# SSD mixer: the normalised residual formed on VectorE instead of GpSimd, and both mask products of the first group in banks of the smaller PSUM pool

## The chip, the core and the metric

The kernel runs on one core of a Trainium2 chip. The core has a matrix engine (TensorE, "PE" in the profile; its weight loads are "PEld"), VectorE ("DVE"), ScalarE ("ACT"), GpSimd ("POOL") and SyncE ("SP"), whose queue issues nearly all DMAs here. Each engine takes its own queue of instructions strictly in the order in which they stand; an instruction that waits holds up everything behind it on that engine. The metric is the device time of one execution in microseconds (us), lower is better.

## What is computed

A trunk of two layers on 512 tokens of width 1024. Each layer is: half a gated feed-forward block, a mixer, a second half block, and a gated embedding. The mixer of layer 0 is a bidirectional SSD (state-space) scan, that of layer 1 is neighbourhood attention. The change lies in the SSD mixer, cut here to what matters:

```python
def ssd_mixer(h, w_in, conv_w, conv_b, dt_bias, a_log, d_skip, norm_g, w_out):   # h = rmsnorm(residual, mix_norm)
    proj = h @ w_in
    z, xbc, dt_raw = jnp.split(proj, [SSD_D_INNER, SSD_D_INNER + SSD_CONV_DIM], axis=-1)
    xbc = jax.nn.silu(centred_depthwise_conv(xbc, conv_w, conv_b))
    xs, b_f, c_f, b_b, c_b = jnp.split(xbc, ...)
    dt = jax.nn.softplus(dt_raw.reshape(bsz, seqlen, 2, SSD_HEADS) + dt_bias)
    y_fwd = ssd_scan(xs, dt[:, :, 0], a[0], grp(b_f), grp(c_f))
    y_bwd = flip(ssd_scan(flip(xs), flip(dt[:, :, 1]), a[1], flip(grp(b_b)), flip(grp(c_b))))
    ...
# in ssd_scan, for each chunk of 128 tokens:
    cb = jnp.einsum('bcqgn,bckgn->bcqkg', cc, bc)                       # the mask products
    scores = cb[..., None] * jnp.exp(jnp.where(lower, seg, -jnp.inf))
```

## The kernel before

Activations stand with features on the partitions: the residual `h` is eight tiles of 128 x 512 (tiles `hs`). An fp32 product is made of three matmuls of rounded parts, high x high (line 278), high x low (281), low x high (282). So every operand is kept as two parts. An activation becomes a pair in a tile `md` by `split()` (lines 301 to 309): a rounded copy on ACT (303, or 306 with a gain) and the remainder on DVE (304, or 307 with a gain). A weight unit of 128 x 1024 is loaded into `wr` by SP, rounded into `wh` by ACT (221), and its remainder goes into `wl` by DVE (223); `wh` and `wl` have three buffers each, and a unit is prepared three products ahead of its use. `gemm()` takes a unit and eight pairs: 24 matmuls of 512 columns into one PSUM bank.

The SSD mixer (`ssd`) first makes the product for dt and the first one of `project(0)` from pairs that carry the gain but not yet the norm's factor, since that factor R (tile `rt`, ACT's copy at line 359) is only known a little later. R is multiplied in afterwards (681 for dt, 748 for the first three products). At the same time the loop at line 685 forms the normalised residual `xn`, which all later projections read: `t` = residual x R on GpSimd (687), then `split()` with the gain (306 on ACT, 307 on DVE), eight times.

`project(gi)` makes eight products for each of eight groups: six go through a convolution (752, four times 756, 759, 760) into `bt`, `ct_` and `xt`, two through a gate (780, 781). `steps()` turns the dt product into step sizes: a transpose on PE (696), a chain of small operations of 256 elements on DVE with two on GpSimd between them (700 to 712), cumulative sums on PE (716, 721), copies on ACT, two more transposes (733), and rows written out to DRAM (`crow`, `vrow`, 738 and 739) that `expo()` reads back (797) for the exponents (800, 803).

`scan(gi)` runs beside the projections of the next group: it transposes tokens (834, copied by ACT at 837), makes the mask products of both directions (845, four matmuls of 128 x 128 each into one bank), multiplies them by the mask on DVE (848), and goes on to the states and the output.

PSUM's eight banks are two pools: `mm` with five and `px` with three. A product waits until the last reader of its bank is done. Before, the mask products took a bank of `mm` for the first direction and one of `px` for the second.

The order of each engine's queue is fixed when the program is built: the framework takes instructions by their place in the code, by dependencies and free buffers and by its own estimates of when things are ready; the code adds a few hints (`issue_after`, `keep_in_program_order`). So an edit in one line can change the order around it on every engine.

Of the kernel before, what the change touches and what calls it, by code (L numbers as in the profile page):

```python
# [11 lines left out]
ALU = mybir.AluOpType  # L12
# [58 lines left out]
def trunk(ctx, tc, A, out):  # L71
    nc = tc.nc
    v, s, g, te, sy = nc.vector, nc.scalar, nc.gpsimd, nc.tensor, nc.sync
# [25 lines left out]
    def md(dt=F32):  # L99
        return bp.tile([P, 2, T], dt, name=nm("md"), tag="md", bufs=24)  # L100
# [7 lines left out]
    def bank(tag, bufs):  # L108
        return ps.tile([P, T], F32, name=nm("ps"), tag=tag, bufs=bufs)

    mm_bank = lambda: bank("mm", 5)
    px_bank = lambda: bank("px", 3)
# [14 lines left out]
    def col(i):  # L127
        return cst[:, i:i + 1]
# [129 lines left out]
    def unit(last=False):  # L258

        while (not last or not ready) and len(ready) < 3 and prep_next():  # L260
            pass
        return ready.pop(0)
# [38 lines left out]
    def split(dst, src, gain):  # L301
        if gain is None:
            cast = s.copy(out=dst[:, 0, :], in_=src)
            split.low = v.tensor_sub(out=dst[:, 1, :], in0=src, in1=dst[:, 0, :])
        else:
            cast = s.activation(out=dst[:, 0, :], in_=src, func=AF.Copy, scale=gain)
            split.low = v.scalar_tensor_tensor(out=dst[:, 1, :], in0=src, scalar=gain, in1=dst[:, 0, :],
                                               op0=ALU.mult, op1=ALU.subtract)
        return cast
# [344 lines left out]
    def ssd(norm, nxt):  # L654
# [8 lines left out]
        hk = list(h)  # L663
# [6 lines left out]
        R = norm.end()  # L670
# [13 lines left out]
        xn = []  # L684
        for k in range(KD):
            t = t2()
            g.tensor_mul(out=t, in0=hk[k], in1=R)  # L687
            xn.append(md(F32R))
            split(xn[k], t, col(norm.gain + k))

        def steps():

# [118 lines left out]
        def scan(gi, bt, ct_, xt, zt, e0):  # L811
# [17 lines left out]
            for c in range(NC):  # L829
                pt = px_bank() if c % 2 == 0 else mm_bank()  # L830
# [9 lines left out]
                yield  # L840
            cbm = []
            for dr in range(2):
                pt = (mm_bank, px_bank)[dr]()
                for c in range(NC):
                    te.matmul(out=pt[:, cs(c)], lhsT=bt[:, dr, cs(c)], rhs=ct_[:, dr, cs(c)], start=True, stop=True)  # L845
                m = sc()
                mk = (M_LE, M_GE)[dr]
                v.tensor_mul(out=m.rearrange("p (c q) -> p c q", c=NC), in0=pt.rearrange("p (c q) -> p c q", c=NC),
                             in1=msk[:, mk:mk + P].unsqueeze(1).to_broadcast([P, NC, P]))
                cbm.append(m)  # L850
# [29 lines left out]
            for st in range(3):  # L880
# [4 lines left out]
                pt = px_bank()  # L885
# [164 lines left out]
        for gi in range(NG):  # L1050
            beside = project(gi + 1) if gi + 1 < NG else out_half()
            sn = scan(gi, *cur, e0)
            if gi == NG - 1:
                prs = pairs_of(range(2))
# [32 lines left out]
        for d in range(KD):  # L1087
            pt, w = mm_bank(), unit(d == KD - 1)
# [15 lines left out]
            else:  # L1104
# [5 lines left out]
                             in1=r2.rearrange(grid, c=64))  # L1110
# [456 lines left out]
```

## Time and profile before

| | |
|---|---|
| time before, median of 3 runs | 2313.22 us (2312.47 to 2314.23) |
| the profiled execution | 2312.72 us; its span from first to last instruction 2310.9 us |
| busy share of the span | PE 99%, DVE 79%, ACT 51%, POOL 15% |
| granted TensorE clock, mean | 0.999 |
| loop of line 687 | 368.0 to 380.7 us, eight POOL instructions, 12.7 us |
| the mask products of the first group (line 845) | at 435.4 us |

Times in the profile are microseconds from the start of the span. A row of the timeline gives start, length, engine, line, operation, the tile written and those read, the shape, how many are merged, and in brackets how long the engine stood idle before it and what ended that. A row of waits gives who waited, for whom, the total, how often, and the longest. Durations of single instructions overlap a little on a full queue: the next starts before the last has ended.

### The profile page before, as it was taken

The numbers are of one execution on the slowest core, as the hardware profiler recorded it, in microseconds if no ns is written. First come the engines' busy times: TensorE is split into PE (matmuls) and PEld (weight loads), VectorE is DVE, ScalarE is ACT, GpSimd is POOL, SyncE is SP. The second block draws the span as 40 slices with busy tenths as digits, with TensorE's granted clock in tenths as the row PEclk, the third lists the DMA queues.
The fourth block names the chain that finished last, engine by engine and source line by source line (L and its number), as shares of the span: only waits on it lengthen the run. The fifth ranks groups of instructions, "written<-read, shape, count | busy, mean of one in ns | idle before, by whom it ended". The sixth has DMA issues, their size and how long they took to land.

```text
span 2310.9 us, 35433 instructions
## 1 busy us (share of the span) xinstructions
PE 2294.1 (99%) x13732; PEld 2027.0 (88%) x13732; DVE 1828.3 (79%) x2613; ACT 1179.8 (51%) x2038; POOL 339.1 (15%) x269
## 2 busy tenths in 40 slices
PE   9999999999999999999999999999999999999999
PEld 8899997888888888999998889999878888999987
DVE  8878868878888958987875897887578859888866
ACT  5433445776767864443445443444446755444452
POOL 0000003255554651000003100000110010000020
PEclk9999999999999999999999999999999999999999
DMA  5323323444444643332223222232557732333222
GB/s 189 118 77 109 105 85 108 160 160 138 145 145 138 189 171 118 102 101 94 90 90 109 102 101 96 93 106 78 169 183 208 228 116 87 110 105 101 87 92 73
DMA packets 105224, 281.69 MB, mean 122 GB/s; under 512 B 13136, under 2 KB 14032, under 8 KB 105056
## 3 DMA queue, kind: packets, MB, share of 16 engines
q1 hardware_dynamic: 104768, 279.30, 37.3%
q8 instruction: 107, 1.75, 0.3%
q14 instruction: 61, 0.50, 0.1%
q10 hardware_dynamic: 288, 0.14, 0.0%
HBM read 259.70 MB, written 13.40 MB: 118 GB/s over the span
## 4 chain that ended last, share of the span: by engine, by line
PE 94%; DVE 3%; ACT 1%; DMA 1%; POOL 1%; issue 0%; SPq 0%; ACTq 0%
PE ps L278 19%; PE ps L281 19%; PE ps L282 19%; PE ps L510 10%; PE ps L509 10%; PE ps L508 10%; PE ps L930 1%; PE ps L889 1%; DVE wl L223 1%; PE ps L910 1%; PE ps L1325 1%; PE ps L1271 1%; DVE t L756 1%; PE ps L834 1%; POOL t L687 1%; PE ps L845 1%
## 5 line engine op out<-in xcount | busy, mean ns | idle before, releaser
L278 PE MATMUL ps<-md,wh 128*128 128x512 f32 (+1 forms) x2032 | 799.4, 394 | 2.6 <-ACT wh L221 1.8
L282 PE MATMUL ps<-md,wl 128*128 128x512 f32 (+1 forms) x2032 | 791.5, 390 | 2.8 <-DVE wl L223 2.8
L281 PE MATMUL ps<-md,wh 128*128 128x512 f32 (+1 forms) x2032 | 792.2, 390 | 0.0
L221 ACT CAST wh<-wr 128x1024 fp32r<-128x1024 f32 (+2 forms) x395 | 351.8, 892 | 491.7 <-PE ps L281 249.8
L223 DVE TENSOR_TENSOR wl<-wr,wh 128x1024 fp32r<-128x1024 f32 (+2 forms) x395 | 418.9, 1062 | 86.4 <-ACT wh L221 84.5
L282 PEld LDWEIGHTS ps<-md,wl 128*128 128x128 f32 x2032 | 382.1, 188 | 85.3 <-DVE wl L223 4.9
L278 PEld LDWEIGHTS ps<-md,wh 128*128 128x128 f32 x2032 | 382.8, 188 | 76.6 <-ACT wh L221 2.3
L281 PEld LDWEIGHTS ps<-md,wh 128*128 128x128 f32 x2032 | 382.8, 188 | 71.6
L221 ACT CAST wh<-md 128x1024 fp32r<-128x1024 f32 x175 | 183.6, 1049 | 322.6 <-PE ps L509 293.7
L332 POOL TENSOR_TENSOR sq<-sq,sq 128x512 f32<-128x512 f32 x71 | 101.0, 1423 | 1636.9 <-ACT sq L328 1632.5
L510 PE MATMUL ps<-sc,wl 128*128 128x256 f32 x980 | 277.6, 283 | 0.8 <-DVE wl L223 0.8
L508 PE MATMUL ps<-sc,wh 128*128 128x256 f32 x980 | 277.0, 283 | 0.8 <-ACT wh L221 0.8
L509 PE MATMUL ps<-md,wh 128*128 128x256 f32 x980 | 277.6, 283 | 0.1
L510 PE MATMUL ps<-md,wl 128*128 128x256 f32 x980 | 277.4, 283 | 0.0
L509 PE MATMUL ps<-sc,wh 128*128 128x256 f32 x980 | 277.3, 283 | 0.0
L508 PE MATMUL ps<-md,wh 128*128 128x256 f32 x980 | 277.2, 283 | 0.0
L514 DVE TENSOR_TENSOR t<-ps,t 128x512 f32<-128x512 f32 x245 | 165.9, 689 | 137.3 <-PE ps L510 136.6
L223 DVE TENSOR_TENSOR wl<-md,wh 128x1024 fp32r<-128x1024 f32 x175 | 213.6, 1220 | 16.1 <-ACT wh L221 15.7
L508 PEld LDWEIGHTS ps<-sc,wh 128*128 128x128 f32 x980 | 187.7, 192 | 4.9 <-ACT wh L221 1.0
L509 PEld LDWEIGHTS ps<-sc,wh 128*128 128x128 f32 x980 | 187.8, 192 | 3.8
L509 PEld LDWEIGHTS ps<-md,wh 128*128 128x128 f32 x980 | 188.1, 192 | 1.6 <-DVE md L472 0.4
L508 PEld LDWEIGHTS ps<-md,wh 128*128 128x128 f32 x980 | 188.1, 192 | 1.3
(209 smaller groups left out, 2913.2 us busy)
## 6 DMA issues: line engine op xcount, KB each, us to landing
wr<-in_w_gw_dram SPq DMA_DIRECT2D x70, 512.0 KB, 3.6
md<-in_w_gw_dram SPq DMA_DIRECT2D x70, 512.0 KB, 5.1
wr<-in_w_in_dram SPq DMA_DIRECT2D x65, 512.0 KB, 3.5
wr<-in_w_dn_dram SPq DMA_DIRECT2D x128, 256.0 KB, 2.7
wr<-in_w_gu_dram SPq DMA_DIRECT2D x32, 512.0 KB, 3.5
hs<-crow SPq DMA_DIRECT2D x64, 256.0 KB, 3.6
wr<-in_w_dn_dram SPq DMA_DIRECT2D x32, 384.0 KB, 3.1
wr<-in_w_qkv_dram SPq DMA_DIRECT2D x24, 512.0 KB, 4.3
```

Source lines behind the costliest of these rows:

```text
L221: splits.append(s.copy(out=hi[:, :n], in_=raw[:, :n]))
L223: v.tensor_sub(out=lo[:, :n], in0=raw[:, :n], in1=hi[:, :n])
L278: m = te.matmul(out=pt, lhsT=hi[:, sl], rhs=part(xp, 0, cols), start=first and k == 0, stop=False)
L281: te.matmul(out=pt, lhsT=hi[:, sl], rhs=part(xp, 1, cols), start=False, stop=False)
L282: gemm.last = te.matmul(out=pt, lhsT=lo[:, sl], rhs=part(xp, 0, cols), start=False, stop=last and k == n - 1)
L332: (v if fast else g).tensor_add(out=self.acc, in0=self.acc, in1=q)
L508: te.matmul(out=o, lhsT=hi[:, sl], rhs=xh, start=j == 0 and kk == 0, stop=False)
L509: te.matmul(out=o, lhsT=hi[:, sl], rhs=xl, start=False, stop=False)
L510: te.matmul(out=o, lhsT=lo[:, sl], rhs=xh, start=False, stop=j == 1 and kk == 3)
L514: v.tensor_add(out=k[to], in0=pt, in1=k[other])
L687: g.tensor_mul(out=t, in0=hk[k], in1=R)
L756: v.scalar_tensor_tensor(out=a[:, lo:hi], in0=src[:, lo + o:hi + o], scalar=w(j), in1=a[:, lo:hi], op0=ALU.mult, op1=ALU.add)
```

## The change

The loop that forms `xn` multiplies by gain and factor in one DVE instruction, and `split()` is called without a gain, so it copies and subtracts (303, 304) where it scaled (306, 307). GpSimd does nothing there any more. In `scan`, for group 0, the first direction's mask product takes its bank from `px` like the second; for all other groups nothing changes.

```diff
@@ -684,9 +684,9 @@
         xn = []
         for k in range(KD):
             t = t2()
-            g.tensor_mul(out=t, in0=hk[k], in1=R)
+            v.scalar_tensor_tensor(out=t, in0=hk[k], scalar=col(norm.gain + k), in1=R, op0=ALU.mult, op1=ALU.mult)
             xn.append(md(F32R))
-            split(xn[k], t, col(norm.gain + k))
+            split(xn[k], t, None)
@@ -840,7 +840,7 @@
             cbm = []
             for dr in range(2):
-                pt = (mm_bank, px_bank)[dr]()
+                pt = (mm_bank if gi and dr == 0 else px_bank)()
                 for c in range(NC):
                     te.matmul(out=pt[:, cs(c)], lhsT=bt[:, dr, cs(c)], rhs=ct_[:, dr, cs(c)], start=True, stop=True)
```

The edits move instructions on all queues, but only in the stretch from the loop of line 687 to the projections of group 1. Behind that the queues are the same. The rows below name tiles with the number that the program gives each one: ps_3873, ps_3913, ps_3953, ps_3993 and ps_4027 are the products i = 3 to 7 of `project(0)`, wh_3723/wl_3725 is the weight unit of the first of them, wh_3914/wl_3916 that of ps_3993 and wh_3954/wl_3956 that of ps_4027.

ACT at the start of the stretch, before:

```order
L306 ACTIVATE md_3698<-t_3696,cst 128x512
L306 ACTIVATE md_3703<-t_3701,cst 128x512
L221 CAST wh_3723<-wr_3569 128x1024
L221 CAST wh_3765<-wr_3575 128x1024
L752 ACTIVATE t_3713<-t_3711,ccw 128x512
```

ACT there now:

```order
L359 COPY rt_3648<-ps_3643 128x512
L682 ACTIVATE t_3663<-t_3663,cst 64x512
L221 CAST wh_3723<-wr_3569 128x1024
L303 CAST md_3668<-t_3666 128x512
L303 CAST md_3673<-t_3671 128x512
```

The weight cast wh_3723 has moved from behind the eight scaled copies to ahead of the eight plain casts.

DVE at the same place, before, up to the remainder of that weight:

```order
L307 SCALAR_TENSOR_TENSOR md_3693<-t_3691,cst,md_3693 128x512
L307 SCALAR_TENSOR_TENSOR md_3698<-t_3696,cst,md_3698 128x512
L307 SCALAR_TENSOR_TENSOR md_3703<-t_3701,cst,md_3703 128x512
L748 TENSOR_TENSOR t_3711<-ps_3621,rt_3648 128x512
L223 TENSOR_TENSOR wl_3725<-wr_3569,wh_3723 128x1024
```

DVE there now:

```order
L687 SCALAR_TENSOR_TENSOR t_3696<-hs_84,cst,rt_3648 128x512
L304 TENSOR_TENSOR md_3688<-t_3686,md_3688 128x512
L687 SCALAR_TENSOR_TENSOR t_3701<-hs_85,cst,rt_3648 128x512
L304 TENSOR_TENSOR md_3693<-t_3691,md_3693 128x512
L304 TENSOR_TENSOR md_3698<-t_3696,md_3698 128x512
L304 TENSOR_TENSOR md_3703<-t_3701,md_3703 128x512
L748 TENSOR_TENSOR t_3711<-ps_3621,rt_3648 128x512
L223 TENSOR_TENSOR wl_3725<-wr_3569,wh_3723 128x1024
```

Sixteen instructions instead of eight stand ahead of L748, in an order that mixes products and subtractions.

DVE some 20 us on, around the remainder wl_3916 and L712, the end of the dt chain, before:

```order
L708 SCALAR_TENSOR_TENSOR sc_3814<-sc_3814,sc_3813 128x256
L756 SCALAR_TENSOR_TENSOR t_3797<-t_3795,ccw,t_3797 128x510
L708 SCALAR_TENSOR_TENSOR sc_3814<-sc_3814,sc_3813 128x256
L223 TENSOR_TENSOR wl_3916<-wr_3727,wh_3914 128x1024
L760 SCALAR_TENSOR_TENSOR md_3708<-t_3803,t_3797 128x512
L708 SCALAR_TENSOR_TENSOR sc_3814<-sc_3814,sc_3813 128x256
L756 SCALAR_TENSOR_TENSOR t_3904<-ps_3873,ccw,t_3904 128x510
L709 SCALAR_TENSOR_TENSOR sc_3814<-sc_3814,sc_3812 128x256
L756 SCALAR_TENSOR_TENSOR t_3904<-ps_3873,ccw,t_3904 128x511
L711 SCALAR_TENSOR_TENSOR md_3659<-sc_3814,sc_3811 128x4x64
L756 SCALAR_TENSOR_TENSOR t_3904<-ps_3873,ccw,t_3904 128x511
L712 SCALAR_TENSOR_TENSOR md_3659<-md_3659,ea 128x4x64
```

DVE there now:

```order
L709 SCALAR_TENSOR_TENSOR sc_3814<-sc_3814,sc_3812 128x256
L756 SCALAR_TENSOR_TENSOR t_3797<-t_3795,ccw,t_3797 128x511
L223 TENSOR_TENSOR wl_3916<-wr_3727,wh_3914 128x1024
L756 SCALAR_TENSOR_TENSOR t_3797<-t_3795,ccw,t_3797 128x511
L223 TENSOR_TENSOR wl_3956<-wr_3769,wh_3954 128x1024
L756 SCALAR_TENSOR_TENSOR t_3797<-t_3795,ccw,t_3797 128x510
L223 TENSOR_TENSOR wl_3996<-wr_3878,wh_3994 128x1024
L760 SCALAR_TENSOR_TENSOR md_3708<-t_3803,t_3797 128x512
L711 SCALAR_TENSOR_TENSOR md_3659<-sc_3814,sc_3811 128x4x64
L756 SCALAR_TENSOR_TENSOR t_3904<-ps_3873,ccw,t_3904 128x510
L712 SCALAR_TENSOR_TENSOR md_3659<-md_3659,ea 128x4x64
```

The chain of L708 and L709 now ends ahead of wl_3916, and two more weight remainders stand between wl_3916 and L712.

PE at L716, which reads what L712 writes, before:

```order
L282 MATMUL ps_3993<-md_3683,wl_3916 128x512
L716 MATMUL ps_3833<-md_3659,msk 128x128 x4
L721 MATMUL ps_3840<-md_3659,ones_t 128x256
L278 MATMUL ps_3993<-md_3688,wh_3914 128x512
L281 MATMUL ps_3993<-md_3688,wh_3914 128x512
L733 MATMUL ps_3851<-msk,md_3659 128x128 x2
```

PE there now, first at the start of ps_3993 and then at L716:

```order
L278 MATMUL ps_3993<-md_3668,wh_3914 128x512
L281 MATMUL ps_3993<-md_3668,wh_3914 128x512
L278 MATMUL ps_4027<-md_3668,wh_3954 128x512
L281 MATMUL ps_4027<-md_3668,wh_3954 128x512
L282 MATMUL ps_3993<-md_3668,wl_3916 128x512
```

```order
L282 MATMUL ps_4027<-md_3668,wl_3956 128x512
L278 MATMUL ps_4027<-md_3673,wh_3954 128x512
L281 MATMUL ps_4027<-md_3673,wh_3954 128x512
L716 MATMUL ps_3833<-md_3659,msk 128x128 x4
L721 MATMUL ps_3840<-md_3659,ones_t 128x256
L282 MATMUL ps_4027<-md_3673,wl_3956 128x512
L733 MATMUL ps_3851<-msk,md_3659 128x128 x2
```

L716 has moved from the middle of ps_3993 into ps_4027, and two matmuls of ps_4027 stand ahead of the first one that needs wl_3916.

PE at the mask products (ps_4231 and ps_4238) and the projection ps_4256 behind them, before:

```order
L834 MATMUL ps_4226<-msk,md_3709 128x128 x2
L834 MATMUL ps_4226<-msk,md_3707 128x128
L845 MATMUL ps_4231<-md_3708,md_3707 128x128 x4
L845 MATMUL ps_4238<-md_3708,md_3707 128x128 x4
L278 MATMUL ps_4256<-md_3668,wh_4117 128x512
```

PE there now:

```order
L845 MATMUL ps_4231<-md_3708,md_3707 128x128 x2
L278 MATMUL ps_4256<-md_3668,wh_4117 128x512
```

```order
L278 MATMUL ps_4256<-md_3683,wh_4117 128x512
L281 MATMUL ps_4256<-md_3683,wh_4117 128x512
L845 MATMUL ps_4238<-md_3708,md_3707 128x128 x4
L282 MATMUL ps_4256<-md_3683,wl_4119 128x512
L278 MATMUL ps_4256<-md_3688,wh_4117 128x512
```

The second direction's product has moved from ahead of ps_4256 into the middle of it; both now use the same bank, where before ps_4231 had the bank that ps_4256 takes next.

## The prediction

> **What bounds the kernel now.** First the head of the page: busy time of each engine, then the chain that ended last.
>
> ```profile
> span 2310.9 us, 35433 instructions
> PE 2294.1 (99%) x13732; PEld 2027.0 (88%) x13732; DVE 1828.3 (79%) x2613; ACT 1179.8 (51%) x2038; POOL 339.1 (15%) x269
> PE 94%; DVE 3%; ACT 1%; DMA 1%; POOL 1%; issue 0%; SPq 0%; ACTq 0%
> ```
>
> TensorE (PE) issues almost without a break, so no engine's busy time can be saved one for one. What can be saved is what PE waits, 16.8 us over the span (2310.9 - 2294.1), and what its clock loses after a wait. Both edits lie in the SSD layer, so the second view is the same chain in order of time from 366 to 440 us (columns: start, us, what).
>
> ```profile
> 368.01 12.74 POOL t L687 x8
> ...
> 381.40 1.53 ACT wh L221 x2
> ...
> 407.25 0.34 DVE md L712
> 407.73 1.13 PE ps L716 x8
> ```
>
> The chain leaves PE at 368 us for GpSimd's eight products (L687), goes on through two weight casts behind them on ScalarE, then through VectorE to L712, and is back on PE at L716. The third view is what PE itself waited for between 365 and 440 us (total us, times, longest).
>
> ```profile
> PE ps L282 <- DVE wl L223: 2.3, 2, 1.5
> PE ps L278 <- ACT wh L221: 1.8, 1, 1.8
> PE ps L716 <- DVE md L712: 1.4, 1, 1.4
> PE ps L278 <- DVE sc L848: 0.8, 1, 0.8
> ```
>
> These add up to 6.3 us. The fourth view, PE's timeline, places them and shows a loss that no wait names.
>
> ```profile
> 380.19 0.46 PE L696 MATMUL ps<-msk,t 64*128 64x64 f32 x4
> 382.48 0.50 PE L278 MATMUL ps<-md,wh 128*128 128x512 f32 x1 [1.83 <-ACT wh L221]
> ...
> 384.06 0.50 PE L282 MATMUL ps<-md,wl 128*128 128x512 f32 x1 [0.85 <-DVE wl L223]
> ...
> 384.65 0.63 PE L281 MATMUL ps<-md,wh 128*128 128x512 f32 x1
> 385.08 0.63 PE L282 MATMUL ps<-md,wl 128*128 128x512 f32 x1
> ...
> 388.04 0.40 PE L278 MATMUL ps<-md,wh 128*128 128x512 f32 x1
> 388.28 0.39 PE L281 MATMUL ps<-md,wh 128*128 128x512 f32 x1
> ...
> 403.72 0.50 PE L282 MATMUL ps<-md,wl 128*128 128x512 f32 x1 [1.46 <-DVE wl L223]
> ```
>
> The matmuls from 384.65 to 388.04 start 0.43 us apart, eight of them in 3.39 us, and the later ones 0.23 apart (388.04 to 388.28, and 0.227 on the mean), which would be 1.8: 1.6 us lost to a clock at half speed right after the two waits. All that this stage can give back is therefore 6.3 + 1.6 = **7.9 us**: (a) 1.83 + 0.85 + 1.6 = 4.3 around 380 to 388, (b) 1.46 at 403.7, (c) 1.40 at 407.7, (d) 0.79 at 438.
>
> **The change, part by part.** The first edit empties GpSimd's stretch and gives VectorE (DVE) 16 instructions in place of 8: eight scalar-times-tensor-times-tensor products (L687) and eight subtractions (L304) where eight L307 stood. ScalarE (ACT) gets casts L303 for L306. The DVE rows of before, with one GpSimd row:
>
> ```profile
> 367.96 0.68 DVE L681 TENSOR_TENSOR t<-ps,rt 64x512 f32<-64x512 f32 x1 [1.87 <-ACT rt L359]
> ...
> 371.35 1.45 DVE L307 SCALAR_TENSOR_TENSOR md<-t,cst,md 128x512 fp32r<-128x512 f32 x1 [0.25 <-ACT md L306]
> ...
> 381.52 0.75 DVE L307 SCALAR_TENSOR_TENSOR md<-t,cst,md 128x512 fp32r<-128x512 f32 x1 [0.24 <-ACT md L306]
> 382.19 0.69 DVE L748 TENSOR_TENSOR t<-ps,rt 128x512 f32<-128x512 f32 x1
> 382.79 1.22 DVE L223 TENSOR_TENSOR wl<-wr,wh 128x1024 fp32r<-128x1024 f32 x1
> ```
>
> L307 takes 1.45 us while GpSimd works and 0.75 once it has stopped (381.52). The new forms stand elsewhere in this trace, on the same operands:
>
> ```profile
> L462 DVE SCALAR_TENSOR_TENSOR t<-hs,cst,rt x32: 735/744/755, 38.8 to 1944.0; 128x512 f32<-128x512 f32 x32
> L304 DVE TENSOR_TENSOR md<-t,md x34: 674/684/693, 39.5 to 1953.9; 128x512 fp32r<-128x512 f32 x34
> L303 ACT CAST md<-t x34: 610/622/627, 38.3 to 1952.9; 128x512 fp32r<-128x512 f32 x34
> ```
>
> On a full DVE queue the next instruction starts about 0.08 us before the last one ends (382.19 + 0.69 against 382.79), so I count 0.66 for a product, 0.60 for a subtraction or L748, and 1.14 for a weight remainder (L223).
>
> *(a)* DVE from 367.96: L681 0.60, 8 x 0.66 = 5.28, 8 x 0.60 = 4.80, L748 0.60, which gives 379.24; the remainder wl_3725 ends at 380.46. Its cast wh_3723 no longer stands behind eight dependent ACT instructions but ahead of them, with L682 alone between it and L681, so it ends long before 380. PE is done with L696 at about 380.5, uses wh first and the remainder two matmuls later, at 380.95. Margin 0.5 us: the waits of 1.83 and 0.85 and the half clock go. ACT's casts (0.62 us, so 0.54 apart) stay ahead of the subtractions by some 0.4 us. **(a) becomes 0**; at 0.06 us more for each of the 16, half a microsecond of wait comes back.
>
> *(b)* What is late next is the same engine. Before wl_3916, DVE's new order holds, behind wl_3725: 10 L756, two L223, a reciprocal, two L760, two L748, eight products of 256 elements, three scalar operations of 256. Their prices:
>
> ```profile
> 392.61 1.74 DVE L703 RECIPROCAL sc<-sc 128x256 f32<-128x256 f32 x1
> ...
> 394.84 0.83 DVE L710 TENSOR_SCALAR sc<-sc 128x256 f32<-128x256 f32 x1
> 395.60 1.17 DVE L756 SCALAR_TENSOR_TENSOR t<-t,ccw,t 128x510 f32<-128x510 f32 x1
> 396.68 0.28 DVE L706 TENSOR_SCALAR sc<-sc 128x256 f32<-128x256 f32 x1
> ...
> 398.13 0.42 DVE L708 SCALAR_TENSOR_TENSOR sc<-sc,sc 128x256 f32<-128x256 f32 x1
> 398.46 0.74 DVE L756 SCALAR_TENSOR_TENSOR t<-t,ccw,t 128x510 f32<-128x510 f32 x1
> ```
>
> 10 x 0.66 + 2 x 1.14 + 1.66 + 4 x 0.60 + 8 x 0.33 + 3 x 0.20 = 16.2, and 0.5 because L706 waits for GpSimd's two products, behind 1.2 us of other work; those two take 1.7 us:
>
> ```profile
> 394.52 1.00 POOL L704 TENSOR_TENSOR sc<-sc,sc 128x256 f32<-128x256 f32 x1 [13.79 <-DVE sc L703]
> 395.60 0.62 POOL L705 TENSOR_TENSOR sc<-sc 128x256 f32<-128x256 f32 x1
> ```
>
>  From 380.38 that starts wl_3916 at 397.1 and ends it at 398.3. Beside GpSimd two DVE rows above took longer (1.17 for 0.74, 0.83 for 0.28, together 1.0); with that it ends at 399.3. PE meanwhile runs three units of 24 matmuls and, in the new order, four instead of two matmuls before it needs this remainder: 380.5 + 76 x 0.227 = 397.75. **(b) becomes 0.5 to 1.6; I take 1.1**, the middle, since the same two contended places exist again.
>
> [...]
>
> *(c)* L712 must end before L716. From the start of wl_3916 at 397.6 (middle again) DVE has three L223, three L756, L760, L711 and L712: 3.42 + 1.98 + 0.60 + 0.33 + 0.42 = 6.75, so 404.35. PE reaches L716 25 matmuls after 398.8, at 404.5. **(c) becomes 0.2**: nothing for L716 and a little for L733, which now has one matmul less in front of it to cover ACT's copy L718. Bounds 0 and 0.8.
>
> *(d)* The second edit frees a bank of the larger pool, for which the next projection waited 0.79 us (L278 <- L848), but both mask products now share one bank, so the second one waits for the first one's L848 instead, in PE's queue with the same projection behind it. The trace has no such wait; its bounds are 0 and twice the nearest row, 1.6. **I leave it at 0.8.**
>
> Moved along: the eight writes each of crow and vrow start with L734 and L735, which no longer stand behind a table load; one weight load passes ahead of them on SP; GpSimd's queue has nothing behind L687 but L704, which waited 13.8 us for DVE anyway.
>
> Sum: 7.9 - (0 + 1.1 + 0.2 + 0.8) = **5.8 us saved**. The profiled execution took 2312.72 us, 0.5 below the median 2313.22, so 2306.9 and, on the median, **2307.4**.
>
> **Rivals.**
>
> *The clock falls again.* The granted clock of 385 to 390 us shows the loss in (a), and the stretches after the waits of 1.46 and 1.40 show none:
>
> ```profile
> 385.00:390.00 5.00, 5.00 (x17) 3.95 (x16) 4.77 (x8) 1.64 (x4) 0.00 (x0) 0.70 0.59 210
> 405.00:410.00 5.00, 3.60 (x21) 2.87 (x20) 5.00 (x11) 1.67 (x9) 0.00 (x0) 1.00 0.25 94
> ```
>
> So 2.7 us of waits within 3.4 us halve the clock and 1.5 do not. If (b) comes out at 1.6 or more and meets a bad phase, 1.6 us are lost again: saved 5.8 - 0.5 - 1.6 = 3.7, time 2309.5. [...]
>
> *The hidden transfer comes out.* ACT's new order puts eight exponent instructions (L800, L803), fed by the read of crow, ahead of a weight cast and of the L752 that frees the next projection's bank. Reads of crow landed 4.2 to 6.9 us after issue here:
>
> ```profile
> L797 SPq DMA_DIRECT2D hs<-crow x7: 327/383/688, 420.7 to 427.7; - x7
> DMA to landing us min/median/max: 4.2/6.3/6.9
> ```
>
> ```profile
> 428.84 0.76 ACT L752 ACTIVATE t<-ps,ccw 128x512 f32<-128x512 f32 x1
> ```
>
> That L752 ended at 429.6, 8.5 us ahead of PE's use of the bank at 438.15. PE comes there some 6 us earlier now; ACT, if the read holds it, does not, and then 2.5 us of cover are left, about what a read of 6.9 us instead of 4.2 uses up. With 2 us beyond that, 2309.4.
>
> *The change does not reach PE:* DVE is the bound from 368 to 408 and pays back all it gains, (b) and (c) grow by what (a) loses. Against it: from L681 to L748 DVE spends 14.2 us now (367.96 to 382.19) and 10.7 in the sum of (a), so its own row shrinks too. It would give 2311.5 to 2313.
>
> *Slower.* The new DVE instructions take what L307 took, 1.45 us, because something else than GpSimd slows them. 16 x (1.37 - 0.63) = 11.8 us; PE would wait 11.3 at 381, lose 1.6 of clock, then about 1.1 and 0.8: 14.8 against 7.9, so 2320. The gain is gone from about 0.92 us per instruction and the loss passes 0.2% from 1.21. Against it stands the 0.75 us row at 381.52, after GpSimd's end.
>
> **How the numbers follow.** Forecast, 5 to 7 us saved: 0.56. More than that, (b) and (d) vanish, down to 2305.3: 0.14. Clock or transfer, 2308.6 to 2310.6: 0.20. No effect: 0.06. Slower: 0.04. A measurement of this kernel tells about 0.2% from no change, 4.6 us, so faster means below 2308.6. The range takes in the bounds of b to d and the first two rivals: 2305.0 to 2310.6. Faster 0.71, the same 0.25, slower 0.04.
>
> **What would show it.** Right: no wait on wh or wl near 381 and no stretch at half clock after it; L687 at about 0.74 us on DVE; wl_3916 still the longest wait of the stage, near 1 us; L845 instead of L278 waiting for L848; everything after 470 us shifted by one constant. Wrong: L687 above 0.8 us, a new wait of PE on ACT behind L800 near 430, or a clock below 1.0 anywhere from 380 to 440.

## The result, and the profile after

| | before | after |
|---|---|---|
| median of 7 runs each, taken together | 2313.60 us (2312.47 to 2314.23) | 2305.22 us (2305.06 to 2305.77) |
| ratio | | 0.9965, interval 0.9954 to 0.9975 |
| the profiled execution, its span | 2312.72, 2310.9 us | 2305.77, 2304.0 us |

The change saves 8.4 us by these medians (5.8 to 10.6 by the interval); over 29 later runs the kernel before has a median of 2313.17, which makes it just under 8. The forecast was 5.8. The page's head after, in the order of the three lines shown for before:

```profile
span 2304.0 us, 35426 instructions
PE 2292.0 (99%) x13732; PEld 2025.5 (88%) x13732; DVE 1826.6 (79%) x2621; ACT 1179.0 (51%) x2038; POOL 323.7 (14%) x261
PE 95%; DVE 3%; DMA 1%; ACT 1%; issue 0%; SPq 0%; POOL 0%; ACTq 0%; POOLq 0%
```

GpSimd has left the chain, and PE waits 12.0 us over the span (2304.0 - 2292.0) instead of 16.8. Between 365 and 440 us, where the list of PE's waits had four rows with 6.3 us, it has one:

```profile
PE ps L282 <- DVE wl L223: 0.6, 1, 0.6
```

PE's timeline at the four places (start, length, instruction, idle before it):

```profile
381.38 0.46 PE L696 MATMUL ps<-msk,t 64*128 64x64 f32 x4
381.77 0.50 PE L278 MATMUL ps<-md,wh 128*128 128x512 f32 x1
...
382.33 0.39 PE L282 MATMUL ps<-md,wl 128*128 128x512 f32 x1
...
398.87 0.39 PE L281 MATMUL ps<-md,wh 128*128 128x512 f32 x1
399.88 0.50 PE L282 MATMUL ps<-md,wl 128*128 128x512 f32 x1 [0.62 <-DVE wl L223]
...
405.68 1.05 PE L716 MATMUL ps<-md,msk 128*128 128x128 f32 x8
...
406.82 0.58 PE L282 MATMUL ps<-md,wl 128*128 128x512 f32 x1
407.24 0.40 PE L733 MATMUL ps<-msk,md 128*128 128x128 f32 x2
...
430.14 0.61 PE L845 MATMUL ps<-md,md 128*128 128x128 f32 x4
430.51 0.48 PE L278 MATMUL ps<-md,wh 128*128 128x512 f32 x1
...
433.13 1.05 PE L845 MATMUL ps<-md,md 128*128 128x128 f32 x8
```

Nothing waits at 381 to 383, at L716 or at L845, and behind L696 the matmuls go on without a break, 0.23 us apart from the second on; the clock is 1.00 in every window from 380 to 410 us. VectorE's rows for the same stretch, with how often a merged row repeats at its end:

```profile
369.14 0.68 DVE L681 TENSOR_TENSOR t<-ps,rt 64x512 f32<-64x512 f32 x1 [1.87 <-ACT rt L359]
369.75 2.72 DVE L687 SCALAR_TENSOR_TENSOR t<-hs,cst,rt 128x512 f32<-128x512 f32 x4
372.40 2.48 DVE L304 TENSOR_TENSOR md<-t,md 128x512 fp32r<-128x512 f32 x4
...
379.86 0.68 DVE L748 TENSOR_TENSOR t<-ps,rt 128x512 f32<-128x512 f32 x1
380.46 1.21 DVE L223 TENSOR_TENSOR wl<-wr,wh 128x1024 fp32r<-128x1024 f32 x1
...
387.57 0.62 DVE L760 SCALAR_TENSOR_TENSOR md<-t,t 128x512 f32<-128x512 f32 x1
388.12 0.67 DVE L748 TENSOR_TENSOR t<-ps,rt 128x512 f32<-128x512 f32 x1
389.51 0.29 DVE L706 TENSOR_SCALAR sc<-sc 128x256 f32<-128x256 f32 x1 [0.73 <-POOL sc L705]
...
398.61 1.22 DVE L223 TENSOR_TENSOR wl<-wr,wh 128x1024 fp32r<-128x1024 f32 x1
...
432.28 0.68 DVE L848 TENSOR_TENSOR sc<-ps,msk 128x512 f32<-128x512 f32 x1
```

and GpSimd's next instruction after the loop's place:

```profile
387.82 0.97 POOL L704 TENSOR_TENSOR sc<-sc,sc 128x256 f32<-128x256 f32 x1 [29.38 <-DVE sc L703]
```

The sixteen new instructions take 0.66 and 0.60 us apiece on a full queue, and the first remainder (380.46) ends at 381.67, ahead of the L282 at 382.33 that reads it. None of them is stretched. Neither are L760 and L748, which run beside GpSimd's L704 (387.82 to 388.79); beside its L705 (388.87 to 389.48) VectorE is idle.

One thing in these times is not the change's. The profiled execution after came into the stretch 1.2 us later than the one before, by what happened long ahead of the edits: the program's first L346 stands at 28.45 us before and at 29.20 after, L681 at 367.96 and 369.14. So the stretch itself is measured from L681 to the first L910, the first matmul behind the reordered part, here in the timeline of before and then of after:

```profile
476.39 0.44 PE L910 MATMUL ps<-sc,md 128*64 128x128 f32 x4
```

```profile
469.63 0.55 PE L910 MATMUL ps<-sc,md 128*64 128x128 f32 x6
```

That is 108.43 us before and 100.49 after: **7.9 us saved inside the stretch**. From L910 to the last matmul it is 1829.7 us before (2306.13 - 476.39) and 1829.6 after. Nothing is won or lost behind it.

### The profile page after: what moved, and what is told of

It is laid out like the page before. It is cut to its first block, busy times and chain, and to the rows that moved or that the text cites. A ratio compares the mean times of both kernels' runs of the same rounds, so it can differ in the third digit from the quotient of the medians.

```text
span 2304.0 us, 35426 instructions
## 1 busy us (share of the span) xinstructions
PE 2292.0 (99%) x13732; PEld 2025.5 (88%) x13732; DVE 1826.6 (79%) x2621; ACT 1179.0 (51%) x2038; POOL 323.7 (14%) x261
## 4 chain that ended last, share of the span: by engine, by line
PE 95%; DVE 3%; DMA 1%; ACT 1%; issue 0%; SPq 0%; POOL 0%; ACTq 0%; POOLq 0%
PE ps L278 19%; PE ps L282 19%; PE ps L281 19%; PE ps L510 10%; PE ps L509 10%; PE ps L508 10%; PE ps L930 1%; PE ps L889 1%; PE ps L910 1%; PE ps L1325 1%; PE ps L1271 1%; DVE wl L223 1%; PE ps L845 1%; PE ps L834 1%; DVE md L304 1%; PE ps L1314 0%
## 5 line engine op out<-in xcount | busy, mean ns | idle before, releaser
L278 PE MATMUL ps<-md,wh 128*128 128x512 f32 (+1 forms) x2032 | 798.6, 393 | 0.0
L282 PE MATMUL ps<-md,wl 128*128 128x512 f32 (+1 forms) x2032 | 790.5, 389 | 1.6 <-DVE wl L223 1.6
L223 DVE TENSOR_TENSOR wl<-wr,wh 128x1024 fp32r<-128x1024 f32 (+2 forms) x395 | 418.5, 1061 | 84.4 <-ACT wh L221 82.6
L282 PEld LDWEIGHTS ps<-md,wl 128*128 128x128 f32 x2032 | 381.5, 188 | 83.5 <-DVE wl L223 2.9
L278 PEld LDWEIGHTS ps<-md,wh 128*128 128x128 f32 x2032 | 382.2, 188 | 73.8 <-issue 0.7
L223 DVE TENSOR_TENSOR wl<-md,wh 128x1024 fp32r<-128x1024 f32 x175 | 213.4, 1219 | 16.3 <-ACT wh L221 15.9
```

Of the source, the lines that this page charges most:

```text
L223: v.tensor_sub(out=lo[:, :n], in0=raw[:, :n], in1=hi[:, :n])
L278: m = te.matmul(out=pt, lhsT=hi[:, sl], rhs=part(xp, 0, cols), start=first and k == 0, stop=False)
L282: gemm.last = te.matmul(out=pt, lhsT=lo[:, sl], rhs=part(xp, 0, cols), start=False, stop=last and k == n - 1)
```

## Experiments

The times below are medians; the kernel before has 2313.17 us in the first four and 2313.02 in the next three, whose runs were taken beside them.

### The edits apart

The first edit alone keeps the loop and puts the banks back; the second alone does the reverse.

e1, against the changed kernel:

```diff
-                pt = (mm_bank if gi and dr == 0 else px_bank)()
+                pt = (mm_bank, px_bank)[dr]()
```

e2, against the kernel before:

```diff
-                pt = (mm_bank, px_bank)[dr]()
+                pt = (mm_bank if gi and dr == 0 else px_bank)()
```

> The first edit alone; the mask products take their banks as before. Theory (the two edits work together): the stretch up to 410 us is that of the changed kernel, but behind both mask products the next projection (L278) waits for the first L848 again. In the changed kernel PE is done with the first product at 430.5 us and L848 ends at 432.96; with the second product's four matmuls in front (0.4 us) the wait is about 2.0 us, so 2305.2 + 2.0 = 2307.2. Rival (the wait of 0.79 us fell away because of the first edit's shift, and the second edit is worth nothing): 2305.2, no wait on L848. Second rival (the second edit carries most of the gain): above 2310.

> The second edit alone; GpSimd forms the products as before. Theory: the waits at 381, 403 and 407 us stay as before (1.8, 0.85, 1.5, 1.4), and the second mask product (L845), which now stands six matmuls further on, waits for L848 in place of L278, 0 to 0.9 us, since L848 stands where it stood in DVE's queue: 0 to 1.0 us faster than before, 2312.6 to 2313.6. Rival (the second edit carries the gain): under 2310.

Measured: e1 2307.24 us (2306.82 to 2307.85; ratio 0.9973, 0.9963 to 0.9984), e2 2313.08 us (ratio 1.0000, 0.9991 to 1.0009). PE in e1 at the mask products (two records to a matmul of L845):

```profile
429.51 1.50 PE L845 MATMUL ps<-md,md 128*128 128x128 f32 x12
432.39 0.50 PE L278 MATMUL ps<-md,wh 128*128 128x512 f32 x1 [1.38 <-DVE sc L848]
```

and PE's waits in e2 between 365 and 440 us:

```profile
PE ps L278 <- ACT wh L221: 1.8, 1, 1.8
...
PE ps L845 <- DVE sc L848: 0.6, 1, 0.6
```

The first edit alone saves about 6 us. The second alone saves nothing that can be told from zero: the wait changes its name, from 0.79 at L278 to 0.60 at L845. With the first edit it is worth 2.0 us by the medians (the seven runs of e1 and of after do not overlap) and 1.65 from L681 to L910 in the traces. In e1's order two of the eight mask matmuls stand further ahead, so that 12 records and not 16 are left in front of L278; PE is through with them 0.4 us sooner, L848 is not, and the wait of 0.79 grows to 1.38. The second edit takes it away. Neither rival holds. Two details came out otherwise than expected. The wait in e1 was put at 2.0 us, in part because the four matmuls in front of it were counted at 0.4 and take about 0.8 (433.13 to 433.94 after), so that the median met the 2307.2 in part by luck. And in e2's trace the waits on remainders sum to 1.0 and not to 2.3 us, with the clock at half for 6.8 us (382.9 to 389.7), where before it was for 3.4: part of what PE waited for before was lost to the clock here.

### The place of the weight cast, without the other engine

Against the kernel before:

```diff
-        xn = []
+        xn = []; len(ready) < 3 and prep_next()
```

> The kernel before, except that the next weight unit is prepared ahead of the loop: its cast (L221) and remainder (L223) stand behind the first of the eight scaled copies, and GpSimd goes on forming the products. Theory (the cast's place is one half of it, DVE's time the other): the waits on wh and wl at 382 to 384 us go, and with them the half clock, 4.5 us; but DVE's eight L307 still take 1.45 us each, the dt chain behind them ends as late as before, and PE comes to L716 that much earlier, so the wait on L712 grows from 1.4 to 5 to 7 us: time within 1 us of before, 2312.5 to 2314.5. Rival (the place in ScalarE's queue is all): L716 waits under 2 us and the time is 2309 or less.

Measured: 2315.96 us (ratio 1.0014, 1.0005 to 1.0023). The two longest of PE's waits in e3 over the whole span, then VectorE's group from 368 to 383 us (count, busy us, mean ns, idle before):

```profile
PE ps L716 <- DVE md L712: 6.9, 1, 6.9
PE ps L278 <- DVE sc L848: 2.2, 1, 2.2
```

```profile
L307 DVE SCALAR_TENSOR_TENSOR md<-t,cst,md 128x512 fp32r<-128x512 f32 x8 | 10.9, 1419 | 1.4 <-ACT md L306 1.4
```

The copies that L307 reads, in ScalarE's timeline, one from the middle of the loop before and the last one in e3:

```profile
372.29 0.72 ACT L306 ACTIVATE md<-t,cst 128x512 fp32r<-128x512 f32 x1 [0.97 <-POOL t L687]
```

```profile
381.70 0.73 ACT L306 ACTIVATE md<-t,cst 128x512 fp32r<-128x512 f32 x1 [0.96 <-POOL t L687]
```

The waits on wh and wl near 382 us are gone, as both theories said, and all of it comes back at L716 (6.9 for 1.4). VectorE spends 10.9 us on eight L307, and the dt chain behind them is as late as ever. The time is 1.5 us above the expected range: the clock falls to half from 405.2 to 412.0 us, during the long wait and behind it, and the projection behind the mask products waits 2.2 us instead of 0.8, neither of which was counted. So the cast's place alone does not give the gain; what comes behind the loop on VectorE has to come earlier too. The theory put its lateness down to L307's 1.45 us, but the pace of the loop is GpSimd's. Before, its products start 1.70 us apart, ScalarE waits 0.97 us for each, and VectorE, with its 1.45, still waits 0.24 for the copy. In e3 the last copy waits for GpSimd until 381.70, so the last L307 could not have run much earlier with faster ones ahead of it. The first two products, with VectorE idle for most of their time (368.64 to 370.09 us), take 1.29 and 1.30 us, and the six behind them, beside VectorE's L307, 1.72 to 1.74.

### GpSimd put back beside VectorE

Against the changed kernel:

```diff
-        xn = []
+        xn = []; gx = sq()
...
-            v.scalar_tensor_tensor(out=t, in0=hk[k], scalar=col(norm.gain + k), in1=R, op0=ALU.mult, op1=ALU.mult)
+            v.scalar_tensor_tensor(out=t, in0=hk[k], scalar=col(norm.gain + k), in1=R, op0=ALU.mult, op1=ALU.mult); g.tensor_mul(out=gx, in0=hk[k], in1=R)
```

> The changed kernel with GpSimd's eight products put back beside VectorE's, into a tile that nothing reads: every other queue keeps its order. Theory (two engines on the same memory slow each other): GpSimd's products take about 1.7 us each, 13 us together, and the L687 and L304 beside them go from 0.74 and 0.68 us to about 1.45; some nine of them fit into 13 us where twenty would have, so the remainder for ps_3873 comes 6 us late, PE waits about that long on wl near 382 us, and the time is 2311 to 2313, more if the clock falls. Rival (VectorE is not slowed by GpSimd, the 1.45 us of L307 came from its wait on ScalarE's copies): L687 stays at 0.74 us and the time at 2305.2.

Measured: 2314.74 us (ratio 1.0007, 0.9998 to 1.0015): the whole gain is gone. GpSimd's products in the view of line 687 (min/median/max ns, first and last start), VectorE's groups between 366 and 382 us, PE's wait, and windows of 5 us (PE busy, clock granted, DMA share, GB/s):

```profile
L687 POOL TENSOR_TENSOR sq<-hs,rt x8: 1291/1618/1631, 368.6 to 380.1; 128x512 f32<-128x512 f32 x8
```

```profile
L304 DVE TENSOR_TENSOR md<-t,md 128x512 fp32r<-128x512 f32 x4 | 6.9, 1771 | 0.0
L687 DVE SCALAR_TENSOR_TENSOR t<-hs,cst,rt 128x512 f32<-128x512 f32 x4 | 6.4, 1652 | 0.0
L681 DVE TENSOR_TENSOR t<-ps,rt 64x512 f32<-64x512 f32 x1 | 0.7, 683 | 1.9 <-ACT rt L359 1.9
```

```profile
389.13 0.80 PE L282 MATMUL ps<-md,wl 128*128 128x512 f32 x1 [7.28 <-DVE wl L223]
```

```profile
385.00:390.00 5.00, 0.87 (x2) 0.50 0.00 0
390.00:395.00 5.00, 5.00 (x13) 0.50 0.60 210
```

No other queue has changed its order and no data flows between the two loops, yet L304 goes from 0.68 to 1.77 us and L687 from 0.74 to 1.65. From L681 to L910 it takes 109.98 us instead of 100.49: 7.4 of wait from start to start and 2.8 of half clock (384.9 to 395.1 us, of which PE works from 389.1 on), less the 0.8 at the second remainder, where e4 does not wait. L681, which ran from 368.5 to 369.2 us beside GpSimd's first product and reads one of its operands from PSUM, kept its 0.68. So in this trace L304 and L687, whose operands are tiles in SBUF, are stretched beside GpSimd, and L681 is not; what decides between them is not shown. The rival falls.

### The fold of the gain

Against the changed kernel:

```diff
-            v.scalar_tensor_tensor(out=t, in0=hk[k], scalar=col(norm.gain + k), in1=R, op0=ALU.mult, op1=ALU.mult)
+            v.tensor_mul(out=t, in0=hk[k], in1=R)
...
-            split(xn[k], t, None)
+            split(xn[k], t, col(norm.gain + k))
```

> The changed kernel with the gain left where it was: VectorE multiplies residual and factor without it, and the split scales as before (L306 and L307). GpSimd is idle as in the change, so this is the move between the engines without the fold of the gain. Theory: L307 runs at 0.75 us, not 1.45, and L306 at 0.72 instead of 0.62, so VectorE has 8 x 0.07 = 0.6 us more; but the slower split shifts the built order, the cast for ps_3873 stands behind three copies and its remainder behind a first convolution step. Counted by the rows of the changed kernel (369.1 + 0.6 + 16 x 0.66 + 0.6 + 0.7 for the step, then 1.2 for the remainder) it ends about 383.4 us where PE wants it at 382.0: 1.4 us at the first remainder and up to 0.8 more behind it, 2306.6 to 2308. Rival (the fold is the gain, the engine is not): near before, 2312 or more. Second rival (the fold is worth nothing): 2305.2.

Measured: 2306.49 us (ratio 0.9973, 0.9962 to 0.9984). VectorE's first rows in e5, then the two rows of ScalarE's and of PE's timeline where PE waits:

```profile
369.38 1.88 DVE L687 TENSOR_TENSOR t<-hs,rt 128x512 f32<-128x512 f32 x3
371.18 2.06 DVE L307 SCALAR_TENSOR_TENSOR md<-t,cst,md 128x512 fp32r<-128x512 f32 x3
```

```profile
392.88 0.63 ACT L759 ACTIVATE t<-t 128x512 f32<-128x512 f32 x1 [4.46 <-DVE t L756]
393.42 1.03 ACT L221 CAST wh<-wr 128x1024 fp32r<-128x1024 f32 x1
```

```profile
394.50 0.50 PE L278 MATMUL ps<-md,wh 128*128 128x512 f32 x1 [1.05 <-ACT wh L221]
395.85 0.50 PE L282 MATMUL ps<-md,wl 128*128 128x512 f32 x1 [0.61 <-DVE wl L223]
```

Without the fold 6.5 us of the gain stay; the fold adds 1.3 by the medians and 1.24 from L681 to L910 (101.73). It does so by another way than expected: the plain product is shorter than the scaled one (1.80 us from row to row for three, 0.60 apiece, against 0.66), which pays for the longer L307, so the first remainder is in time. Instead a later weight cast stands behind an L759 that waits 4.5 us for VectorE's convolution, and PE waits 1.05 for it. The size was nearly as expected, its place was not. In this order L710 and an L756 stand beside GpSimd's L704 and L705 and take 0.83 and 1.17 us, as they did before the change; in the changed kernel they do not.

### VectorE loaded with more

Against the changed kernel:

```diff
-            v.scalar_tensor_tensor(out=t, in0=hk[k], scalar=col(norm.gain + k), in1=R, op0=ALU.mult, op1=ALU.mult)
+            [v.scalar_tensor_tensor(out=t, in0=hk[k], scalar=col(norm.gain + k), in1=R, op0=ALU.mult, op1=ALU.mult) for _ in range(1 + (k >= 4))]
```

> The changed kernel with the last four products of the loop formed twice on VectorE (4 x 0.66 = 2.6 us more, same values). In the changed kernel the remainder for ps_3873 ends at 381.7 us and PE uses it at 382.0, a margin of 0.3 us. Theory (VectorE's queue sets the stretch, nothing absorbs it): all but 0.3 of the 2.6 us comes back as waits on remainders (L223) between 381 and 405 us, 2307.5, and 0.5 to 1.6 more where the clock falls. Rival (VectorE has slack there): within 0.5 us of 2305.2.

Measured: median 2310.53 us (ratio 0.9985, 0.9976 to 0.9993), but the eleven times lie apart: four from 2307.6 to 2308.5, one at 2309.5, six from 2310.5 to 2311.0. The mean clock on record is 0.999 for those six and 1.000 for the other five, so the one at 2309.5, which the expectations below count with the upper group, is not explained by the clock. The profile was of the lowest group. In it PE waits 2.8 us, against 0.6, and takes 103.28 us from L681 to L910, 2.8 more than the change: all of the added 2.6 comes back, and VectorE has no slack there (the queues of ScalarE and PE change their order in a few places too). The place was misjudged: the first remainder costs 0.37 us, and 2.17 come at 401.9, on the remainder that still waits in the changed kernel. To see what parts the groups, the same kernel was profiled twice more.

> The kernel with four products twice once more, for a second profile: its eleven times lie in two groups, 2307.6 to 2308.5 and 2309.5 to 2311.0, and the one profile is of the lower group (clock 1.00 throughout). Theory (the clock is granted in steps of about 3.4 us that do not stand still against the program, so the same waits cost it in some executions and not in others): an execution near 2310.5 has the same waits (2.2 us at 382, 2.8 in all) and one or two stretches of about 3.4 us at 0.5 that begin within 4 us of the long wait; 3.4 us of a busy PE at half speed are 1.7 us. Rival (the two groups differ in the waits themselves, by a transfer or the start): an execution near 2310.5 shows another wait of 2 us or more, and a clock of 1.00.

> The same kernel and the same expectation as the look before: near 2308.3 with the clock at 1.00 throughout, or near 2310.5 with the same waits and a stretch at half clock behind the wait of 2.2 us.

Measured: 2310.28 and 2310.47 us. Windows of one us in e6 (us, PE busy with matmuls, clock granted, DMA share, GB/s):

```profile
402.00:403.00 1.00, 1.00 (x5) 1.00 0.19 37
403.00:404.00 1.00, 1.00 (x6) 1.00 0.77 254
```

and in e9, with the same wait:

```profile
401.88 0.80 PE L282 MATMUL ps<-md,wl 128*128 128x512 f32 x1 [2.17 <-DVE wl L223]
```

```profile
402.00:403.00 1.00, 1.00 (x3) 0.50 0.08 16
403.00:404.00 1.00, 1.00 (x4) 0.50 0.72 254
...
405.00:406.00 1.00, 1.00 (x5) 0.85 0.90 242
```

The same instructions and the same wait to 0.01 us, once at full clock and once at half for about 3.4 us (and so in e8): 104.84 and 104.85 us from L681 to L910 in e8 and e9, 1.6 more than in e6. The theory holds in what it says of the waits and of the time at half clock, with the wait at 402 us, not at 382 as its text says. Of its steps the traces show this: before, the half clock lasts 3.413 us (384.593 to 388.006), and the next change, at 2309.71 us, comes 563 times that length on. In e9 the clock falls at 401.90, and the whole wait (399.71 to 401.88) lies in the 3.4 us ahead of that; so it does in e8 (399.86 to 402.02, the fall at 402.16). Whether its place decides is not shown: in e6 no fall marks where a step would end. How much idle time halves the clock is not settled: in e2 PE had stood idle for 1.74 us (381.11 to 382.85) when it fell.

### One product back on GpSimd

A try at the 0.62 us that are left. Against the changed kernel:

```diff
-            v.scalar_tensor_tensor(out=t, in0=hk[k], scalar=col(norm.gain + k), in1=R, op0=ALU.mult, op1=ALU.mult)
+            g.tensor_mul(out=t, in0=hk[k], in1=R) if k == 7 else v.scalar_tensor_tensor(out=t, in0=hk[k], scalar=col(norm.gain + k), in1=R, op0=ALU.mult, op1=ALU.mult)
...
-            split(xn[k], t, None)
+            split(xn[k], t, col(norm.gain + k) if k == 7 else None)
```

> The changed kernel with the last of the eight products back on GpSimd, and scaled in its split; a try at the wait of 0.62 us that is left. Theory: VectorE saves one product (0.66 us), and GpSimd's one product of 1.3 to 1.7 us slows one or two VectorE instructions beside it by 0.9 each, so nothing is won: 2304.7 to 2306. Rival (each product taken off VectorE is won up to the remaining 0.8 us): 2304.4. Second rival (one product suffices to bring the contention back at the place that matters): 2307 or more.

Measured: 2306.44 us (2305.58 to 2307.86; ratio 0.9971, 0.9960 to 0.9982), 1.2 above the change and 0.4 above the expected range. From L681 to L910 it is 101.60 us, 1.1 more. GpSimd in e7's timeline, VectorE's rows at the end of its product, and its eight products before in the view of line 687:

```profile
373.36 4.87 POOL L687 TENSOR_TENSOR t<-hs,rt 128x512 f32<-128x512 f32 x1 [15.32 <-DVE md L304]
```

```profile
377.00 0.68 DVE L748 TENSOR_TENSOR t<-ps,rt 128x512 f32<-128x512 f32 x1
377.61 1.78 DVE L304 TENSOR_TENSOR md<-t,md 128x512 fp32r<-128x512 f32 x2
```

```profile
L687 POOL TENSOR_TENSOR t<-hs,rt x8: 1291/1735/1744, 368.0 to 379.0; 128x512 f32<-128x512 f32 x8
```

The one product took 4.87 us, where before the longest of eight took 1.74. The two engines did not share the loss: VectorE's instructions beside the product kept their 0.68 and 0.74 us up to L748, which reads PSUM, at 377.00. From there to the product's end at 378.23 are 1.23 us, about what one takes alone (1.29), and the L304 that starts in this time takes 0.5 us longer. So of the 0.9 us for one or two VectorE instructions only 0.5 came. PE then waits 0.83 and 0.61 near 394 us. The 0.83 is for a weight cast behind an L759 that waits 4.7 us for VectorE's convolution, as in e5: the cost comes through the new order. Nothing is won; no version that was tried beats the change.

## Why the prediction was right, and where its sizes were off

The mechanism held at (a), (b) and (c) but not at (d). The time came out 2.2 us below the forecast and inside the range by 0.2 only. 7.9 us saved are more than the 5 to 7 that had a chance of 0.56; they lie at the end of the branch with 0.14, in which (b) and (d) vanish. In fact (d) vanished and (b) halved. By terms, with the loss counted from start to start of PE's matmuls beside the idle time that the list of waits names:

| | named before | start to start before | forecast left | left after, start to start |
|---|---|---|---|---|
| (a) 381 to 388 us | 1.83 + 0.85 + 1.6 | 4.5 | 0 | 0 |
| (b) remainder wl_3916 | 1.46 | 1.6 | 1.1 | 0.8 (0.62 named) |
| (c) L716, L733 | 1.40 | 1.6 | 0.2 | 0 |
| (d) mask products | 0.79 | 1.0 | 0.8 | 0 |
| sum | 7.9 | 8.7 | 2.1 | 0.8 |

From start to start that is 8.7 - 0.8 = 7.9, as measured from L681 to L910. No wait is left in (c): L733 starts 0.42 us behind the matmul that follows L721, and the instruction in that place took the same 0.42 before the change (408.94 to 409.36).

- **(d) is the term that failed.** "I leave it at 0.8" carried the wait over to L845 by its name and never timed it, although the rows shown for the change held the answer: eleven matmuls of 512 columns stand between the two products. After, they fill 430.51 to 433.13 us, and L848 ends at 432.96, 0.17 us ahead of the L845 that needs the bank. So the step that failed is the one from a new name to an unchanged wait: nothing waits for L848 any more. With five matmuls between them (e2) 0.60 of wait is left; in e1, with only the second product's matmuls ahead of the L278 that waits, 1.38.
- **(b) was too high** because the slowed VectorE instructions beside GpSimd's two products were taken to recur. In the new order L760, L748 and idle time stand there, and none is stretched (0.62 and 0.67 us above). In e5, where L710 and an L756 do stand there, they are slowed as priced (0.83 and 1.17 us). The 0.8 are the lower bound of 0.5 and 0.3 more, mainly because VectorE loses 0.8 us to GpSimd's pair (388.12 to 389.51, of which 0.6 are L748) and not 0.5.
- **The total was too small.** The named waits understate the loss here: the 1.83 at L278 moves its start by 1.90 (380.19 to 382.48 before, 381.38 to 381.77 after), and the 0.62 at L282 costs 0.78 (1.01 from 398.87 to 399.88 where 0.23 is usual). Over five waits that is the 0.8 between the second and the third column.
- **(a)** became 0 as predicted. e3 shows that the cast's place alone is not enough, since the gain goes back at L716, and e4 that GpSimd must be silent, since VectorE's new work gives the gain back when GpSimd runs beside it. That the cast has to stand ahead of the copies is not shown: no run leaves it behind all eight with the new products. An estimate from the rows after says that it may not have to: ScalarE is done with the last L303 at 378.78, and a cast of 1.04 us behind it would end near 379.8, ahead of the 380.46 at which L223 reads it. The forecast put the first remainder 11.3 us behind the start of L681; it is at 380.46 - 369.14 = 11.32.
- **The signs and the rivals.** No wait for wh or wl near 381, the full clock, L687 at 0.74 us and one constant shift behind 470 us were as announced; the wait of L845 for L848 was not. The clock did not fall in the changed kernel (1.00 from 380 to 440 us), where no wait above 0.62 is left in the stretch; behind a wait of 2.2 us on the same remainder it fell in e8 and e9 and not in e6. The read of crow held ScalarE for 0.5 us at 419.7, but no matmul waited for it. The slower case was shut out by L687 at 0.74 us; in e4, where half of the sixteen are slowed, the whole gain is gone.

## What to carry to other kernels

A wait that changes its name has to be timed again: count what stands between the two instructions in the new order, and set it against the length of the work that is waited for. Work moved from GpSimd to a VectorE that looks full can shorten VectorE's own stretch: here its eight instructions took twice their time beside GpSimd (1.45 us for 0.75), and came at GpSimd's pace, one in 1.70 us. Read the same form beside and away from GpSimd before costing it. And hoisting a late cast alone only moved the wait to the next instruction that the late engine feeds (here L716, 6.9 us of wait for 1.4).

## What the runs showed of the hardware that was not expected

- In these traces the half clock lasts 3.4 us or two or three times that, and does not stand at one place of the program: 3.4 us before (384.6 to 388.0), 6.8 in e2 (382.9 to 389.7) and in e3 (405.2 to 412.0), 10.2 in e4 (384.9 to 395.1), and behind the same wait of 2.2 us 3.4 in e8 and e9 and none in e6. The runs of e6 are spread over 3.4 us, of which the traces give 1.6 to the clock, and those of the changed kernel over 0.7.
- Which of VectorE and GpSimd pays for working side by side differed between the runs. In e4 both did: eight products of 1.62 us at the median beside VectorE instructions of 1.65 and 1.77, which take 0.74 and 0.68 in the changed kernel. In e7 GpSimd did nearly alone: 4.87 us for one product, 0.5 us lost on VectorE. VectorE's queue was full in both, so its fullness is not the reason; what decides which of the two is slowed stays open.
